# Rotary embedding: float32 transfers on the SyncE hardware queue, with ScalarE doing the casts

## The chip, the cores and the metric

The kernel runs on one core of a Trainium2 chip. The metric is the device time of one execution in microseconds (us). A profile's span is about 1.8 us shorter than the time of the same execution (317.2 us against 319.0 us for the kernel before), because the time also holds what lies outside the first and last recorded instruction.

## The reference

`x` has shape (8, 2048, 16, 64), in float32. The two halves of its last dimension are rotated by angles that depend on the sequence position alone:

```python
x1, x2 = x[..., :32], x[..., 32:]
out1 = x1 * cos - x2 * sin          # cos, sin: (2048, 32), broadcast over batch and heads
out2 = x1 * sin + x2 * cos
return np.concatenate([out1, out2], axis=-1).astype(np.float32)
```

The kernel must read 67.1 MB and write 67.1 MB of float32. There is very little arithmetic per byte, so the transfers will matter most.

## The kernel before

One tile holds a batch: 128 partitions x 16 positions x 16 heads x 64 values, in float16. GpSimd issues every transfer on its software queue, and the transfer itself casts between float32 in HBM and float16 in SBUF. VectorE works in place in float16. There are five such tiles.

```python
def load(b):
    xt = io_pool.tile([P, J, H, D], f16)                    # io_pool: bufs=5, J = 16
    nc.gpsimd.dma_start(out=xt, in_=x[b].rearrange("(p j) h d -> p (j h d)", j=J))
    return xt

def rotate(xt):
    for j0 in range(0, J, JC):                              # JC = 8
        # ... views x1, x2, sin_b, cos_b, xw; temporaries v1, v2
        nc.vector.tensor_mul(out=v1, in0=x2, in1=sin_b)
        nc.vector.tensor_mul(out=v2, in0=x1, in1=sin_b)
        nc.vector.tensor_mul(out=xw, in0=xw, in1=cos_b)     # both halves at once
        nc.vector.tensor_sub(out=x1, in0=x1, in1=v1)
        nc.vector.tensor_add(out=x2, in0=x2, in1=v2)

for b in range(B):
    tiles[b] = load(b)
    # ... the tables with b == 0
    if b >= 4:
        nc.gpsimd.dma_start(out=out[b - 4].rearrange(...), in_=tiles[b - 4])
    rotate(tiles[b])
# ... the last four stores
```

The build reorders what an engine has to do: it is not bound to the order of the program where no data depends on it.

## Time and profile before

| | before |
|---|---|
| time, median of 6 runs | 319.06 us (318.79 to 319.14) |
| span of the profiled run | 317.2 us |
| VectorE (DVE) busy | 210.7 us, 66% |
| transfers, share of 16 engines' span | 99.6% |
| HBM bytes over the span | 425 GB/s |

From the page of the kernel before: the span, the busy time of each engine with its share of the span and its number of instructions, the busy tenths of the transfers in 40 slices, then the queues with packets, MB and share of 16 engines.

```profile
span 317.2 us, 164 instructions
DVE 210.7 (66%) x80; POOL 9.9 (3%) x22
DMA  7979999999999999999999999999999999999996
q0 software_dynamic: 2592, 100.93, 99.6%
q14 instruction: 1, 0.01, 0.0%
HBM read 67.63 MB, written 67.11 MB: 425 GB/s over the span
```

The queue is full from end to end. Mind the MB column: a packet is counted by one side only, so a casting load counts its float16 bytes (33.5 MB) and a casting store its float32 bytes (67.1 MB). The HBM line counts float32 both ways.

The windows view of the same kernel, first and last stretch (window, length, busy time of VectorE and GpSimd with the number of instructions, clock, share of the transfers, GB/s):

```profile
0.00:20.00 20.00, 0.00 (x0) 4.05 (x11) 1.00 0.89 184
280.00:317.00 37.00, 0.00 (x0) 0.00 (x0) 1.00 0.93 397
```

Only about 2 us at the start (11% of 20) and 2.6 us at the end (7% of 37) are not streaming. Two waits (engine, line, what it waited for: us, times, longest) tell the rest:

```profile
POOL xt L37 <- DMA out_dram<-xt: 118.1, 3, 56.4
DVE v L55 <- DMA xt<-in_x_dram: 29.9, 2, 20.2
```

GpSimd stands in three waits for a store to land before it may load into that tile again, and VectorE waits for loads. Neither costs anything as long as the queue has work.

### The profile page before, as it was taken

The numbers are of one execution on the slowest core, as the hardware profiler recorded it, in microseconds if no ns is written. First come the engines' busy times: TensorE is split into PE (matmuls) and PEld (weight loads), VectorE is DVE, ScalarE is ACT, GpSimd is POOL, SyncE is SP. The second block draws the span as 40 slices with busy tenths as digits, with TensorE's granted clock in tenths as the row PEclk, the third lists the DMA queues.
The fourth block names the chain that finished last, engine by engine and source line by source line (L and its number), as shares of the span: only waits on it lengthen the run. The fifth ranks groups of instructions, "written<-read, shape, count | busy, mean of one in ns | idle before, by whom it ended". The sixth has DMA issues, their size and how long they took to land.

```text
span 317.2 us, 164 instructions
## 1 busy us (share of the span) xinstructions
DVE 210.7 (66%) x80; POOL 9.9 (3%) x22
## 2 busy tenths in 40 slices
DVE  0009999999999999999069999995009994000000
POOL 5000000000000000001000000100000000000000
DMA  7979999999999999999999999999999999999996
GB/s 132 256 163 266 207 198 202 260 198 198 198 264 264 397 397 529 397 331 231 231 198 199 380 413 397 454 471 264 198 314 413 397 446 479 397 397 512 413 397 264
DMA packets 2593, 100.93 MB, mean 318 GB/s; under 512 B 288, under 2 KB 544, under 8 KB 544
## 3 DMA queue, kind: packets, MB, share of 16 engines
q0 software_dynamic: 2592, 100.93, 99.6%
q14 instruction: 1, 0.01, 0.0%
HBM read 67.63 MB, written 67.11 MB: 425 GB/s over the span
## 4 chain that ended last, share of the span: by engine, by line
issue 34%; DMA 19%; DVE 16%; another core or an unknown queue 13%; POOL 1%; POOLq 0%; DVEq 0%; PEldq 0%
DMA xt<-in_x_dram 12%; DMA sin_sb<-in_sin_dram 7%; DVE xt L58 5%; DVE v L55 3%; DVE xt L60 3%; DVE v L56 3%; DVE xt L59 2%; POOL xt L37 1%; POOL out_dram L68 1%; POOLq L101 0%; POOLq L37 0%; POOLq L73 0%; DVEq L55 0%; PEldq L101 0%
## 5 line engine op out<-in xcount | busy, mean ns | idle before, releaser
L55 DVE TENSOR_TENSOR v<-xt,sin_sb 128x4096 f16<-128x4096 f16 x16 | 36.5, 2284 | 54.2 <-DMA xt<-in_x_dram 29.9
L58 DVE TENSOR_TENSOR xt<-xt,cos_sb 128x8192 f16<-128x8192 f16 x16 | 70.7, 4416 | 0.0
L59 DVE TENSOR_TENSOR xt<-xt,v 128x4096 f16<-128x4096 f16 x16 | 36.5, 2283 | 0.1
L60 DVE TENSOR_TENSOR xt<-xt,v 128x4096 f16<-128x4096 f16 x16 | 36.5, 2283 | 0.0
L56 DVE TENSOR_TENSOR v<-xt,sin_sb 128x4096 f16<-128x4096 f16 x16 | 36.5, 2283 | 0.0
L37 POOL DMA_DIRECT2D xt<-in_x_dram x8 | 4.4, 568 | 118.9 <-DMA out_dram<-xt 118.1
L68 POOL DMA_DIRECT2D out_dram<-xt x4 | 2.1, 539 | 73.8 <-DVE xt L60 73.8
L73 POOL DMA_DIRECT2D out_dram<-xt x4 | 2.1, 532 | 63.0 <-DVE xt L60 63.0
L44 POOL DMA_DIRECT2D cos_sb<-in_cos_dram x1 | 0.5, 548 | 0.0
L43 POOL DMA_DIRECT2D sin_sb<-in_sin_dram x1 | 0.5, 542 | 0.0
L90 POOL MEMSET const-float32-0.0<- 128x1 f32 x1 | 0.1, 100 | 0.2 <-issue 0.2
L90 POOL MEMSET const-bfloat16-1.0<- 128x1 bf16 x1 | 0.1, 103 | 0.0
L90 POOL MEMSET const-float32-1.0<- 128x1 f32 x1 | 0.1, 100 | 0.0
L90 POOL MEMSET const-uint8-127<- 128x1 uint8 x1 | 0.1, 100 | 0.0
## 6 DMA issues: line engine op xcount, KB each, us to landing
xt<-in_x_dram POOLq DMA_DIRECT2D x8, 4096.0 KB, 39.8
sin_sb<-in_sin_dram POOLq DMA_DIRECT2D x1, 128.0 KB, 22.2
cos_sb<-in_cos_dram POOLq DMA_DIRECT2D x1, 128.0 KB, 22.4
out_dram<-xt POOLq DMA_DIRECT2D x8, 65.9
```

The costliest lines, as they stand in the source:

```text
L37: nc.gpsimd.dma_start(out=xt, in_=x[b].rearrange("(p j) h d -> p (j h d)", j=J))
L43: nc.gpsimd.dma_start(out=sin_sb, in_=sin.rearrange("(p j) d -> p (j d)", j=J))
L44: nc.gpsimd.dma_start(out=cos_sb, in_=cos.rearrange("(p j) d -> p (j d)", j=J))
L55: nc.vector.tensor_mul(out=v1, in0=x2, in1=sin_b)
L56: nc.vector.tensor_mul(out=v2, in0=x1, in1=sin_b)
L58: nc.vector.tensor_mul(out=xw, in0=xw, in1=cos_b)
L59: nc.vector.tensor_sub(out=x1, in0=x1, in1=v1)
L60: nc.vector.tensor_add(out=x2, in0=x2, in1=v2)
L68: nc.gpsimd.dma_start(out=out[b - 4].rearrange("(p j) h d -> p (j h d)", j=J), in_=tiles[b - 4])
L73: nc.gpsimd.dma_start(out=out[b].rearrange("(p j) h d -> p (j h d)", j=J), in_=tiles[b])
L90: nc = _bacc.Bacc("TRN2", target_bir_lowering=False, num_devices=1)
```

## The change

The intent: the hardware queue in place of the software queue, plain float32 rows of 32 KB in place of casting rows of 64 KB, and the casts on ScalarE, which had nothing to do. Core of the diff:

```diff
-    JC = 8
+    JU = 8                                   # positions in a transfer: 32 KB rows, 4 MB tiles
+    JC = 4                                   # positions in a piece of compute
+    NBUF = 5
     def load(u):
-        xt = io_pool.tile([P, J, H, D], f16)
-        nc.gpsimd.dma_start(out=xt, in_=x[b].rearrange("(p j) h d -> p (j h d)", j=J))
+        xf = io_pool.tile([P, JU, H, D], f32)
+        nc.sync.dma_start(out=xf.rearrange("p j h d -> p (j h d)"), in_=rows(x, b, j0))
+    def narrow(c):                            # half_pool: bufs=3
+        xt = half_pool.tile([P, JC, H, D], f16)
+        nc.scalar.copy(out=xt.rearrange("p j h d -> p (j h d)"), in_=piece(c))
     # ... rotate: the same five VectorE operations, on half tiles of JC = 4
+    def widen(c):                             # back into the input tile
+        nc.scalar.copy(out=piece(c), in_=xt.rearrange("p j h d -> p (j h d)"))
+    # ... the first four loads and the tables, narrow(0)
+    for c in range(n * per):                  # n = 16 units, per = 2 pieces each
+        if c + 1 < n * per:
+            narrow(c + 1)
+        rotate(c)
+        widen(c)
+        if c % per == per - 1:
+            u = c // per
+            if u + NBUF - 1 < n:
+                tiles[u + NBUF - 1] = load(u + NBUF - 1)   # waits until store(u - 1) has landed
+            store(u, tiles[u])
```

More of the change, by code (lines that the diff above doesn't have):

```diff
@@ L20 @@
     f16 = mybir.dt.float16
+    f32 = mybir.dt.float32
     B, S, H, D = x.shape
@@ L25 @@
     J = S // P
-    JC = 8
+    JU = 8
+    JC = 4
+    NBUF = 5
     const_pool = ctx.enter_context(tc.tile_pool(name="rope_const", bufs=1))
-    io_pool = ctx.enter_context(tc.tile_pool(name="rope_io", bufs=5))
-    tmp_pool = ctx.enter_context(tc.tile_pool(name="rope_tmp", bufs=2))
+    io_pool = ctx.enter_context(tc.tile_pool(name="rope_io", bufs=NBUF))
+    half_pool = ctx.enter_context(tc.tile_pool(name="rope_half", bufs=3))
+    tmp_pool = ctx.enter_context(tc.tile_pool(name="rope_tmp", bufs=1))
@@ L32 @@
+    cos_f = const_pool.tile([P, J, Dh], f32)
+    sin_f = const_pool.tile([P, J, Dh], f32)
     cos_sb = const_pool.tile([P, J, Dh], f16)
     sin_sb = const_pool.tile([P, J, Dh], f16)
-    def load(b):
-        xt = io_pool.tile([P, J, H, D], f16)
-        nc.gpsimd.dma_start(
-            out=xt, in_=x[b].rearrange("(p j) h d -> p (j h d)", j=J)
-        )
-        return xt
-    def tables():
-        nc.gpsimd.dma_start(out=sin_sb, in_=sin.rearrange("(p j) d -> p (j d)", j=J))
-        nc.gpsimd.dma_start(out=cos_sb, in_=cos.rearrange("(p j) d -> p (j d)", j=J))
@@ L46, in rotate @@
-    def rotate(xt):
-        for j0 in range(0, J, JC):
-            js = slice(j0, j0 + JC)
-            v1 = tmp_pool.tile([P, JC, H, Dh], f16)
-            v2 = tmp_pool.tile([P, JC, H, Dh], f16)
-            x1 = xt[:, js, :, 0:Dh]
-            x2 = xt[:, js, :, Dh:D]
-            sin_b = sin_sb[:, js, :].unsqueeze(2).to_broadcast([P, JC, H, Dh])
-            cos_b = cos_sb[:, js, :].unsqueeze(2).to_broadcast([P, JC, 2 * H, Dh])
-            nc.vector.tensor_mul(out=v1, in0=x2, in1=sin_b)
-            nc.vector.tensor_mul(out=v2, in0=x1, in1=sin_b)
-            xw = xt[:, js, :, :].rearrange("p j h (e d) -> p j (h e) d", d=Dh)
-            nc.vector.tensor_mul(out=xw, in0=xw, in1=cos_b)
-            nc.vector.tensor_sub(out=x1, in0=x1, in1=v1)
-            nc.vector.tensor_add(out=x2, in0=x2, in1=v2)
@@ L62 @@
-    tiles = {}
-    for b in range(B):
-        tiles[b] = load(b)
-        if b == 0:
-            tables()
-        if b >= 4:
-            nc.gpsimd.dma_start(
-                out=out[b - 4].rearrange("(p j) h d -> p (j h d)", j=J), in_=tiles[b - 4]
-            )
-        rotate(tiles[b])
-    for b in range(B - 4, B):
-        nc.gpsimd.dma_start(
-            out=out[b].rearrange("(p j) h d -> p (j h d)", j=J), in_=tiles[b]
-        )
+    units = [(b, j0) for b in range(B) for j0 in range(0, J, JU)]
@@ new lines, in rows, with load, store @@
+    def rows(t, b, j0):
+        return t[b].rearrange("(p j) h d -> p j (h d)", j=J)[:, j0 : j0 + JU, :].rearrange(
+            "p j f -> p (j f)"
+        )
+    def load(u):
+        b, j0 = units[u]
+        xf = io_pool.tile([P, JU, H, D], f32)
+        nc.sync.dma_start(out=xf.rearrange("p j h d -> p (j h d)"), in_=rows(x, b, j0))
+        return xf
+    def store(u, xf):
+        b, j0 = units[u]
+        nc.sync.dma_start(out=rows(out, b, j0), in_=xf.rearrange("p j h d -> p (j h d)"))
@@ new lines, with piece, rotate @@
+    n = len(units)
+    per = JU // JC
+    tiles = {}
+    halves = {}
+    def piece(c):
+        u, k = divmod(c, per)
+        return tiles[u][:, k * JC : (k + 1) * JC, :, :].rearrange("p j h d -> p (j h d)")
+    def narrow(c):
+        xt = half_pool.tile([P, JC, H, D], f16)
+        nc.scalar.copy(out=xt.rearrange("p j h d -> p (j h d)"), in_=piece(c))
+        halves[c] = xt
+    def rotate(c):
+        u, k = divmod(c, per)
+        j0 = units[u][1] + k * JC
+        js = slice(j0, j0 + JC)
+        xt = halves[c]
+        v1 = tmp_pool.tile([P, JC, H, Dh], f16)
+        v2 = tmp_pool.tile([P, JC, H, Dh], f16)
+        x1 = xt[:, :, :, 0:Dh]
+        x2 = xt[:, :, :, Dh:D]
+        sin_b = sin_sb[:, js, :].unsqueeze(2).to_broadcast([P, JC, H, Dh])
+        cos_b = cos_sb[:, js, :].unsqueeze(2).to_broadcast([P, JC, 2 * H, Dh])
+        nc.vector.tensor_mul(out=v1, in0=x2, in1=sin_b)
+        nc.vector.tensor_mul(out=v2, in0=x1, in1=sin_b)
+        xw = xt.rearrange("p j h (e d) -> p j (h e) d", d=Dh)
+        nc.vector.tensor_mul(out=xw, in0=xw, in1=cos_b)
+        nc.vector.tensor_sub(out=x1, in0=x1, in1=v1)
+        nc.vector.tensor_add(out=x2, in0=x2, in1=v2)
@@ new lines, in widen @@
+    def widen(c):
+        xt = halves.pop(c)
+        nc.scalar.copy(out=piece(c), in_=xt.rearrange("p j h d -> p (j h d)"))
+    for u in range(NBUF - 1):
+        tiles[u] = load(u)
+        if u == 0:
+            nc.sync.dma_start(out=sin_f, in_=sin.rearrange("(p j) d -> p j d", j=J))
+            nc.sync.dma_start(out=cos_f, in_=cos.rearrange("(p j) d -> p j d", j=J))
+            nc.scalar.copy(out=sin_sb, in_=sin_f)
+            nc.scalar.copy(out=cos_sb, in_=cos_f)
+    narrow(0)
+    for c in range(n * per):
[8 more added lines that the diff above has]
+            store(u, tiles[u])
```

## The prediction

> **What bounds the kernel now.** The transfers. The page's queue section gives the one software queue 99.6% of 16 engines' span; VectorE is busy 210.7 of 317.2 us (66%). HBM reads and writes are 67.63 + 67.11 MB, 425 GB/s over the span. About 2 us at the start (window 0 to 20 us: DMA share 0.89) and 2.6 us at the end (280 to 317: 0.93) are not streaming, so while streaming it moves about 134.7 MB in 313 us = 430 GB/s. The Trainium skill, "DMA: Bandwidth & Descriptors", section "Where 436 GB/s comes from", puts the ceiling of the 16 ports at 435 GB/s. The trace agrees: the kernel sits 1% below it. VectorE's waits (54 us) are off the critical path.
>
> **What the change removes.** The cast in the transfer and GpSimd's work, but no HBM byte: x and out were float32 in HBM before. On the SBUF side the bytes double, but the float32 side already set the pace (loads and stores both run near 430 GB/s counted in float32: 240 to 280 us shows 436 GB/s, mostly stores). So the gain is at most that 1%, plus about 1 us of start.
>
> **What it adds.** ScalarE: 32 narrowings and 32 widenings of 128x4096. No trace has one; the Trainium skill, "ScalarE: Activation LUTs", section "What ACT_TABLE_LOAD costs", gives 186 ns + 0.833 ns per element, an estimate of 3.6 us each, 230 us in all. VectorE keeps 211 us: per 4 MB unit 13.2 us on VectorE, 14.4 us on ScalarE, against 2 x 4.19 MB / 430 GB/s = 19.5 us of transfer. Compute stays hidden.
>
> **What it moves: the risk.** Half as much is in flight: five tiles of 4 MB, not 8. Load u+5 must wait until store u has landed, on the same in-order SyncE queue as the stores. If the build puts load u+5 ahead of store u+1, as the program has it, then SyncE stands in that wait while store u+1 is ready, and the queue runs empty at each of 11 loads. Each costs landing + issue + first byte, by the start and end losses above about 2.3 us: 25 us, 340 us in all. If the order is store u+1 first (before's trace shows such a reordering: stores 0 and 1 both were issued before load 5), a store covers each wait and nothing is lost: 315 to 318 us. I give both about half, with mixtures between them.
>
> Start: first 4 MB land at 12 us, tables follow, first store at about 35 us while five loads stream until about 52 us; no hole. End: behind the last load about four stores (39 us) cover the last unit's 20 us of compute; no hole.
>
> **Prediction:** 320 us, range 312 to 343; faster by over 2% 0.09, within 2% 0.54, slower by over 2% 0.37.
>
> **What would show each step.** DMA queue: one hardware queue with 134 MB at 96 to 100% of the span if right. ScalarE busy near 230 us, a narrowing 3.6 us; VectorE unchanged at 211 us. Issues: the order of loads and stores on SyncE, and in the waits how long SyncE stands for stores; DMA share near 0.98 or near 0.9 (holes).
>
> **What would make it wrong.** The hardware queue with float32 on both sides streams clearly slower or faster than 430 GB/s; table transfers in tiny pieces (several us at the start); ScalarE, in order, stands at a narrowing whose load hasn't landed while a widening is ready, so that stores come late; copies above 4.8 us, when ScalarE would set the pace.

## More of the kernel before

The trace has a record for each row that a DMA engine moves. The records do not name the engine: a row is joined to the one whose end meets its start, and the spacing is the mean over rows that nothing delays (how the delayed ones are left out moves it by about half a nanosecond). A row of 64 KB (float32 side) starts 2412.8 ns after the one before it on its engine. Sixteen engines at that pace move 16 x 65,536 B / 2412.8 ns = 435 GB/s. The Trainium skill, "DMA: Bandwidth & Descriptors", section "Where 436 GB/s comes from", gives 435 GB/s as the ceiling of the 16 ports; the trace agrees.

## The result, and the profile after

| | before | after |
|---|---|---|
| time, median of 6 runs | 319.06 us | 321.52 us (320.18 to 321.71) |
| ratio, 95% interval | | 1.0067 (1.0047 to 1.0086) |

A ratio is the mean time of one kernel's fast runs over the mean of the other's in the same rounds, so it is not quite the ratio of the medians. The change makes the kernel slower by a small amount that is clear of noise. The runs of after fall in two groups, 320.2 to 320.4 us (two) and 321.5 to 321.7 us (four). The trace kept is one of the first group (span 318.6 us).

The page of the kernel after, the lines that answer to those above:

```profile
span 318.6 us, 387 instructions
DVE 223.2 (70%) x160; ACT 229.3 (72%) x67; POOL 0.2 (0%) x4
DMA  8999999999999999999999999999999999999994
q1 hardware_dynamic: 4896, 134.74, 98.7%
q14 instruction: 3, 0.02, 0.0%
HBM read 67.63 MB, written 67.11 MB: 423 GB/s over the span
```

The queue is still full, now with plain float32 bytes. The costliest groups of after (busy us, mean ns of one, then idle before them and what ended it):

```profile
L92 ACT CAST xf<-xt 128x4096 f32<-128x4096 f16 x32 | 115.3, 3604 | 51.0 <-DVE xt L88 28.0
L69 ACT CAST xt<-xf 128x4096 f16<-128x4096 f32 x32 | 114.5, 3600 | 18.7 <-DMA xf<-in_x_dram 18.7
```

A cast takes 3.60 us. The Trainium skill, "ScalarE: Activation LUTs", section "What ACT_TABLE_LOAD costs", gives 186 ns + 0.833 ns per element for an ACTIVATE with immediate scale and bias, which is 3598 ns for 4096; the trace, which calls the operation CAST, agrees. ScalarE's 229 us and VectorE's 223 us both stay under the transfers.

The order of issue was the disputed step. Timeline of SyncE in after (start, length of the group from its first to its last issue, line, what, how many):

```profile
2.11 2.01 SPq L51 DMA_DIRECT2D xf<-in_x_dram  x4
34.91 18.17 SPq L56 DMA_DIRECT2D out_dram<-xf  x2
63.52 10.26 SPq L51 DMA_DIRECT2D xf<-in_x_dram  x2
73.87 4.33 SPq L56 DMA_DIRECT2D out_dram<-xf  x2
102.56 10.13 SPq L51 DMA_DIRECT2D xf<-in_x_dram  x2
112.74 1.09 SPq L56 DMA_DIRECT2D out_dram<-xf  x2
```

The build issues in pairs: stores 0 and 1, then loads 5 and 6, and so on. Load 5 waits for store 0, but store 1 is then already in the queue, and load 6 waits for store 1 while load 5 is under way. So SyncE's waits are long, but the queue holds work throughout. The windows view of after, in columns as above with ScalarE added, shows no hole between the ends:

```profile
160.00:210.00 50.00, 34.53 (x25) 38.87 (x11) 0.00 (x0) 1.00 1.00 431
210.00:260.00 50.00, 38.38 (x29) 38.80 (x11) 0.00 (x0) 1.00 1.00 434
310.00:318.00 8.00, 0.00 (x0) 0.00 (x0) 0.00 (x0) 1.00 0.58 250
```

The last window, with 0.58 of 16 engines busy, does not set after apart: before has 0.50 in the same window.

**Where the time came from.** The ends of single engines show it. A transfer ends with 16 marks in the trace, one from each DMA engine. The last transfer of before has its first and last mark 0.62 us apart; the last of after has them 2.65 us apart. At the end of after, 15 engines have ended their last row by 315.60 us and one ends its last row at 317.35 us, a row and a half later. I call such an engine a straggler. The kernel ends with its slowest engine. Worked out from the two profiled runs (span 317.2 and 318.6 us):

| term | before | after | difference |
|---|---|---|---|
| first row starts, us from the span's start | 2.61 | 1.74 | -0.9 |
| 128 x 64 KB: row spacing 2412.8 ns, or 2 x 1209.7 ns | 308.8 | 309.7 | +0.9 |
| first to last mark of the last transfer | 0.62 | 2.65 | +2.0 |
| last mark to end of span | 1.5 | 0.9 | -0.6 |
| sum of these | | | +1.4 |

The spans differ by 1.4 us. These terms are not the whole span: they leave 3.7 us over in each kernel, which hold the tables (about 1.3 us) and what all engines lose at their first rows and at the first stores. So the question for the experiments is what makes the straggler.

### The profile page after: what moved, and what is told of

Read it like the earlier page. It is cut to its first block, busy times and chain, and to the rows that moved or that the text cites. A ratio compares the mean times of both kernels' runs of the same rounds, so it can differ in the third digit from the quotient of the medians.

```text
span 318.6 us, 387 instructions
## 1 busy us (share of the span) xinstructions
DVE 223.2 (70%) x160; ACT 229.3 (72%) x67; POOL 0.2 (0%) x4
## 4 chain that ended last, share of the span: by engine, by line
DMA 51%; ACT 7%; DVE 4%; issue 2%; SPq 1%; DVEq 0%; ACTq 0%
DMA out_dram<-xf 45%; DMA xf<-in_x_dram 6%; ACT xf L92 3%; ACT xt L69 3%; DVE xt L86 1%; DVE xt L87 1%; DVE v L83 1%; DVE v L84 1%; DVEq L138 0%; SPq L51 0%; SPq L56 0%; DVE xt L88 0%; ACTq L92 0%
## 5 line engine op out<-in xcount | busy, mean ns | idle before, releaser
L92 ACT CAST xf<-xt 128x4096 f32<-128x4096 f16 x32 | 115.3, 3604 | 51.0 <-DVE xt L88 28.0
L69 ACT CAST xt<-xf 128x4096 f16<-128x4096 f32 x32 | 114.5, 3600 | 18.7 <-DMA xf<-in_x_dram 18.7
L83 DVE TENSOR_TENSOR v<-xt,sin_sb 128x2048 f16<-128x2048 f16 x32 | 39.1, 1223 | 70.6 <-ACT xt L69 53.6
L86 DVE TENSOR_TENSOR xt<-xt,cos_sb 128x4096 f16<-128x4096 f16 x32 | 73.3, 2292 | 1.2
L87 DVE TENSOR_TENSOR xt<-xt,v 128x2048 f16<-128x2048 f16 x32 | 39.2, 1225 | 1.1
L84 DVE TENSOR_TENSOR v<-xt,sin_sb 128x2048 f16<-128x2048 f16 x32 | 39.0, 1218 | 0.0
L88 DVE TENSOR_TENSOR xt<-xt,v 128x2048 f16<-128x2048 f16 x32 | 39.0, 1218 | 0.0
```

Of the source, the lines that this page charges most:

```text
L69: nc.scalar.copy(out=xt.rearrange("p j h d -> p (j h d)"), in_=piece(c))
L92: nc.scalar.copy(out=piece(c), in_=xt.rearrange("p j h d -> p (j h d)"))
```

## The experiments

In what follows, marks that are "x us apart" are the first and last mark of the last transfer. First theory A: the transfers bind; the loss is the smaller rows and a straggler that the longer program's instruction fetches make (the transfers of 8 KB on the queue that the page calls instruction, q14 above: three in after, one in before). Rival B: compute is late and leaves holes. Each timed run has a 95% interval of at most 0.25% to either side, against the kernel before of the same rounds.

### e1: less compute

```diff
-        nc.vector.tensor_mul(out=v1, in0=x2, in1=sin_b)
-        nc.vector.tensor_mul(out=v2, in0=x1, in1=sin_b)
         nc.vector.tensor_mul(out=xw, in0=xw, in1=cos_b)
-        nc.vector.tensor_sub(out=x1, in0=x1, in1=v1)
-        nc.vector.tensor_add(out=x2, in0=x2, in1=v2)
```

> The changed kernel with one of VectorE's five operations (the cosine product), so a wrong result on purpose; VectorE's busy time falls from 223 to about 75 us and its program from 162 to about 34 instructions. Theory A (the transfers bind; the loss is made of row pieces of 32 KB, about 1 us, and of one DMA engine of the 16 that ends 1.8 us behind the others, late because the instruction fetches of a longer program fall on it): transfers as before, 128 x 2.42 us per engine; fewer fetches than the 3 of the changed kernel, last engine under 1 us behind, 318 to 321 us. Theory B (stores come late, because they wait for rotate and widen, and leave holes): the holes go, 314 to 316 us.

Measured: 320.79 us (319.08 to 321.49), ratio 1.0047. VectorE fell from 223 to 73 us and the time by less than 1 us. Rival B is out: taking away two thirds of VectorE's work returns next to nothing. From its page:

```profile
span 317.5 us, 238 instructions
DVE 73.3 (23%) x32; ACT 227.3 (72%) x67; POOL 0.2 (0%) x4
q1 hardware_dynamic: 4896, 134.74, 99.1%
```

There were two fetches, and the last transfer's marks lay 1.44 us apart in place of 2.65; theory A had expected less than 1.

### e2: pieces of half the size

```diff
-    JC = 4
+    JC = 2
```

> Pieces of half the size (JC 2): the same bytes and transfers, twice the compute instructions (320 on VectorE, 128 on ScalarE). Theory A: ScalarE 242 us, VectorE 245 us, both under the 315 us of transfers, so no loss from them; about twice the 3 instruction fetches, so the last engine ends 1 to 2 us further behind: 321.5 to 324 us. If the fetches have nothing to do with the straggler: 320.2 to 321.7 us, as the changed kernel.

Measured: 322.31 us, ratio 1.0105; VectorE 239 us, ScalarE 242 us, four fetches; marks 4.90 us apart. In the range of theory A. But one fetch more moved the marks by 2.25 us, which is much for a record of 0.3 us. The marks of each transfer in turn show part of it: they widen by 0.7 us across the fetch at 57.1 us and by 1.0 us across the one at 238.1 us. e6 puts a price on a fetch.

### e3: rows of 16 KB

```diff
-    JU = 8
-    NBUF = 5
+    JU = 4
+    NBUF = 10
```

> Rows of 16 KB, ten tiles of 2 MB in place of five of 4 MB. Theory A: a row costs a fixed part; before moved 64 KB in 2411 ns start to start and the changed kernel two rows of 32 KB in 2419 ns, so four rows of 16 KB should take 2435 ns, 128 times that is 2 us more: 322.5 to 324 us. If 32 KB rows cost nothing by themselves: 320 to 322 us.

Measured: 330.47 us, ratio 1.0362: a miss. The row's fixed cost is only part of it: rows start 607 ns apart, so 64 KB take 2428 ns against 2419 ns, and 128 times 9 ns is 1.2 us. But the change did more than I meant. The windows view of e3 near its end:

```profile
300.00:312.00 12.00, 8.29 (x7) 8.32 (x4) 0.00 (x0) 1.00 1.01 431
312.00:318.00 6.00, 5.65 (x4) 2.61 (x2) 0.00 (x0) 1.00 0.70 296
318.00:324.00 6.00, 0.00 (x0) 3.40 (x1) 0.00 (x0) 1.00 0.62 262
```

With the queue nearly empty, the last two stores come late behind their widenings (ScalarE starts its last two at 310.80 and 317.80 us), and all engines have two holes of about 2.1 us. Rows also took longer in many places than their usual 611 ns (mean 627 ns, which is 8 us over the 512 rows of an engine). The marks show where. Averaged over the 16 engines, the transfer that ends a pair of loads, just before stores follow, lands 0.2 to 1.4 us late at each of eleven places about 20 us apart, 6.6 us in all; in after the same sum over six places is about 0.6 us. So the two holes (4.1 us) and these losses are the larger part of e3's 9 us over after, and the size of the row is the smaller. Why halving the transfers made all engines lose there is not shown.

### e4: the order that the prediction feared

```diff
+        with tc.issue_after(issued[-1].ins):       # each store behind the load before it
             nc.sync.dma_start(out=rows(out, b, j0), in_=xf.rearrange(...))
```

> Forces the issue order that the prediction feared: each store behind the load that the program has ahead of it, so SyncE stands in the wait of load u+5 while store u+1 is ready. Both theories: 11 holes. By the prediction's estimate of 2.3 us each 25 us more, 345 us, DMA busy near 91% of the span. If the queue isn't drained (stores late anyway), under 330 us.

Measured: 362.07 us, ratio 1.1347. The waits of SyncE and the queue in e4:

```profile
SPq L53 <- DMA out_dram<-xf: 253.0, 11, 28.4
```

```profile
q1 hardware_dynamic: 4896, 134.74, 93.0%
```

All 11 holes are there, at (362.07 - 321.52) / 11 = 3.7 us each. The row records of a typical one: the last row of a store ends at 86.54 us, the store's last mark is at 86.88, SyncE issues at 86.89, the next rows start at 87.85 and the first takes about 1.9 us instead of 1.2. The mean start of a row is late by 1.9 us at the first row and by 0.6 at the second, 2.5 us together: close to the 2.3 us that I took from the ends of before. Another 1.3 us come where the short queue goes from that load to its store (0.5 and 0.8 us on the mean engine); this cycle is 3.8 us longer than one without a hole. So the mechanism was right, and its price was too low by this second part.

### e5: the software queue put back

```diff
-        nc.sync.dma_start(...)        # x, out, cos, sin
+        nc.gpsimd.dma_start(...)
```

> The changed kernel with every transfer issued by GpSimd (software queue), still float32 and 32 KB rows: the queue alone is put back. If the loss of the changed kernel is its hardware queue: back to 318.5 to 319.5 us, last engine under 0.7 us behind, as before. If it is the rows of 32 KB and the instruction fetches: not faster than the changed kernel, and the start 0.9 us later: 321 to 323 us.

Measured: 324.93 us, ratio 1.0185; marks 4.30 us apart. The hardware queue is not what costs time: without it the kernel is slower still, by more than I expected. The two profiled spans differ by 4.1 us: the first row starts 0.9 us later, the marks lie 1.7 us further apart, and from the last mark to the end of the span it takes 2.1 us in place of 0.9.

### e6: more instruction fetches, and nothing else

```diff
         rotate(c)
+        for _ in range(20):
+            nc.gpsimd.memset(scratch, 0.0)       # one column that nobody reads
         widen(c)
```

> The changed kernel plus 640 memsets of one column on GpSimd, which nothing waits for: transfers, ScalarE's and VectorE's programs unchanged; about 5 instruction fetches of 8 KB more than the 3 of the changed kernel, in the first 65 us. If a fetch costs the DMA engine that serves it about 1 us and that engine is the last: last engine 5 to 9 us behind, 324 to 328 us. If e2's loss came from its smaller pieces, or a fetch costs only the 0.3 us of its record: 320.2 to 322 us.

Measured: 322.99 us, ratio 1.0125, under the range: a half miss. There were eight fetches:

```profile
q14 instruction: 8, 0.07, 0.1%
```

The marks of the transfers widen right where the fetches are: from 0.94 to 1.57 us across the one at 31.3 us (after has 0.48 us there), from 1.55 to 2.73 us across the one at 51.3 us, whose record is the longest with 0.94 us (after goes from 0.48 to 0.54 us there), and from 3.25 to 3.91 us across two at 91.4 and 92.0 us. At the end they are 4.74 us apart, 2.1 us more than in after for five additional fetches. So a fetch can put an engine back by 0.3 to 1.1 us. It shows in the marks only where it meets an engine that is among the last: those of e6 at 179.0 and 294.7 us widen the marks by less than 0.1 us.

The same reading of after and e1, which issue in the same order: the marks of e1 go from 0.42 to 1.44 us, and its two fetches (204.7 and 286.2 us) widen them by no more than 0.05 us. So about 1.0 us of spread comes without fetches. Those of after go from 0.49 to 2.65 us. Its fetch at 292.5 us takes them from 1.89 to 2.68; the one at 91.7 us falls in a stretch where they widen by 0.5 us, against 0.2 us in e1; the one at 179.0 us does nothing. Of the 2.2 us by which the marks of after widen, an estimate from these numbers gives about half to fetches and half to something else. The next runs show what that is.

### c32 and c64: the copy alone, rows of 32 and 64 KB

Both only copy x to out through float32 tiles on the hardware queue: no tables, no compute, a wrong result. In all the copies each issue is pinned behind the one before it (`tc.issue_after`), so the order is that of the program.

```diff
+    # c32: JU = 8, NBUF = 5 (4 MB tiles)        c64: JU = 16, NBUF = 3 (8 MB tiles)
+    tiles = {u: load(u) for u in range(NBUF)}
+    store(0)
+    for u in range(1, n):
+        store(u)
+        if u - 1 + NBUF < n:
+            tiles[u - 1 + NBUF] = load(u - 1 + NBUF)
```

> Copy of x to out through SBUF alone (wrong result on purpose): float32, hardware queue, rows of 32 KB, five tiles of 4 MB, no tables (1.3 us of transfer less), next to no compute program, so 0 or 1 instruction fetches. Theory A: rows start to start 1209.5 ns, last engine under 0.7 us behind, 316 to 318 us. If the hardware queue makes a straggler by itself: still 1.5 us or more behind, 319 us or more.

> The same copy with rows of 64 KB and three tiles of 8 MB. Theory A (a row has a fixed cost of about 8 ns): 2411 to 2413 ns start to start instead of 2 x 1209.5, 1 us less than the 32 KB copy: 315 to 317 us. If the row size costs nothing: same as the 32 KB copy within 0.3 us.

Measured: c32 320.32 us (marks 3.91 us apart), c64 318.70 us (marks 3.07). Neither has a single instruction fetch, and both have stragglers. Theory A falls as the whole cause: there is another source. The row records say where. In c64 the rows of some engines are late by 0.2 to 0.8 us at 120, 159, 198, 238 and 277 us, every 39 us. These are the places where the queue goes from a load to a store (the marks of load 3 end at 120.7 us, those of load 4 at 159.6 us). Where it goes from a store to a load, half way between, little is lost (at most 0.44 us, on one engine at 181 us). In after such losses come near 92, 131, 170 and 209 us, every 39 us, at the end of each pair of loads. Row size by itself: 2 x 1209.5 = 2419.0 against 2414.2 ns, so 0.6 us over 128.

Theory C: at a turn from load to store some engines lose a few tenths of a microsecond, and never catch up. With the cast the SBUF side moves half the bytes, and this hides the turn. That the cast hides it is tested next; that the halved bytes are the reason is not.

### c64g, and the cast with five and with three tiles

```diff
-        nc.sync.dma_start(...)                     # c64
+        nc.gpsimd.dma_start(...)                   # c64g: the same copy on the software queue
-        xf = io_pool.tile([P, JU, H, D], f32)      # c64g
+        xf = io_pool.tile([P, JU, H, D], f16)      # casting copies, NBUF = 5 and NBUF = 3
```

> The 64 KB copy (float32, three tiles of 8 MB) issued by GpSimd in place of SyncE. Theory C (new, after the copies on the hardware queue showed stragglers of 3 to 4 us without any instruction fetch: where the queue turns between loads and stores, float32 on both sides makes some engines lose 0.2 to 0.5 us each time; with the cast the SBUF side moves half the bytes and hides it): as on the hardware queue, stalls every 39 us, last landing 2 to 4 us behind the first, 319 to 322 us with a start 0.9 us later. If the stalls belong to the hardware queue: under 0.7 us behind, 318 us or less.

> The same copy with float16 tiles, so the transfers cast as those of the kernel before, five tiles. Theory C: no stalls at the turns, last landing under 0.7 us behind the first, 315.5 to 317.5 us, 2 us or more under the float32 copy on the same queue. If the cast has nothing to do with it: within 0.5 us of the float32 copy on this queue.

Measured: float32 320.53 us (marks 3.22 us apart), casting with five tiles 317.49 us (marks 0.69). But five tiles also allow fewer turns (4 from load to store in place of 6) and a deeper queue than three. The control with three tiles has the same transfers in the same order as c64g; only the tile's type differs.

> The casting copy with three tiles instead of five, so that its 16 transfers stand in the same order, with the same number of turns and the same depth of queue, as those of the float32 copy on GpSimd (320.53 us); the tile type is the only difference. Theory C (float32 on both sides makes the stalls at the turns): no stalls behind the first one, last landing under 0.8 us behind the first, 317.3 to 318.0 us. Rival D (fewer turns or a deeper queue were what helped the five-tile copy, not the cast): last landing 2 to 3.5 us behind the first, 319.5 us or more.

Measured: 317.65 us, ratio to before 0.9961 (0.9947 to 0.9974); marks 0.73 us apart. Rival D falls. The windows of the float32 copy on GpSimd (window, length, GpSimd, clock, share of the transfers, GB/s):

```profile
308.00:312.00 4.00, 0.00 (x0) 1.00 1.02 442
312.00:316.00 4.00, 0.00 (x0) 1.00 0.23 98
```

and of the casting copy with the same order:

```profile
308.00:312.00 4.00, 0.00 (x0) 1.00 1.22 524
312.00:316.00 4.00, 0.00 (x0) 1.00 0.01 0
```

In the float32 copy a few engines still run when most have ended; the casting copy stops at once. In the row records of c64g one engine is late by 0.6 us at 199, 1.0 us at 239 and 0.9 us at 279 us. In the casting copy no engine is late by as much as 0.2 us after the first turn at 62 us, where all 16 lose about 1.1 us with the cast and 1.3 us without, on average. The row spacing differs by only 1.4 ns (2414.2 and 2412.8), 0.2 us in all.

### c32g3: the same copy, turning less often

```diff
-    store(0)
-    for u in range(1, n):
-        store(u)
-        if u - 1 + NBUF < n:
-            tiles[u - 1 + NBUF] = load(u - 1 + NBUF)
+    for g in range(0, n, 3):
+        for u in range(g, min(g + 3, n)):
+            store(u)
+        for u in range(g + NBUF, min(g + NBUF + 3, n)):
+            tiles[u] = load(u)
```

> The 32 KB copy on the hardware queue with stores and loads in threes rather than one by one: a third of the turns. Theory C: last landing 1 to 2 us behind the first instead of 3.9, 318 to 319.3 us against 320.3. If the turns have no part: 320 to 320.6 us.

Measured: 317.23 us against 320.32 us for c32; marks 0.91 us apart in place of 3.91. The queues of c32 and of c32g3, same bytes and packets:

```profile
q1 hardware_dynamic: 4608, 134.22, 98.4%
```

```profile
q1 hardware_dynamic: 4608, 134.22, 99.2%
```

With 5 turns from load to store in place of 12 the straggler goes, and with it 3.1 us, somewhat more than I expected. The range said a third; it is 5 of 12. The grouping also puts more transfers in the queue ahead of each turn, so the number of turns and the depth of the queue are not told apart here.

### The copies side by side

| kernel | queue | in SBUF | row | turns, load to store | fetches | marks of the last transfer apart | median |
|---|---|---|---|---|---|---|---|
| cast, 3 tiles | GpSimd | float16 | 64 KB | 6 | 0 | 0.73 us | 317.65 us |
| c64g | GpSimd | float32 | 64 KB | 6 | 0 | 3.22 us | 320.53 us |
| c64 | SyncE | float32 | 64 KB | 6 | 0 | 3.07 us | 318.70 us |
| c32 | SyncE | float32 | 32 KB | 12 | 0 | 3.91 us | 320.32 us |
| c32g3 | SyncE | float32 | 32 KB | 5 | 0 | 0.91 us | 317.23 us |
| before | GpSimd | float16 | 64 KB | 3 | 1 | 0.62 us | 319.06 us |
| after | SyncE | float32 | 32 KB | 7 | 3 | 2.65 us | 321.52 us |

Read from the top, each step is one part of the change: float32 in SBUF +2.9 us, the hardware queue -1.8 us, rows of 32 KB with more turns +1.6 us. A grouped order gives 3.1 us back. Some of these runs were made in different rounds and on different chips; by their ratios to the kernel before of the same rounds (318.8 to 319.0 us) the steps are +2.6, -1.6, +1.5 and -2.8 us. What the hardware queue gains lies mostly at the ends: in c64 the first row starts 0.9 us earlier than in c64g, and the span ends 0.6 us sooner after the last mark. The kernels at the bottom also load the tables (0.5 MB, about 1.3 us at this rate) and have a program to fetch. No version that computes the result and beats before was found. A grouped order in the kernel itself was not run, because even a copy that computes nothing is at most 0.6% faster than before. So that grouping would help the computing kernel is not shown.

## Why the prediction was right or wrong

- **"What bounds the kernel now: the transfers."** Right. In e1 VectorE lost two thirds of its work and the time moved by less than 1 us.
- **"So the gain is at most that 1%."** Right, and nothing of it came. The start was 0.9 us earlier as foreseen, but a row pair of 32 KB costs 2419.4 ns in place of 2412.8 (+0.9 us).
- **"ScalarE: an estimate of 3.6 us each, 230 us in all."** Right: 3.60 us and 229.3 us. VectorE has 223 us, not 211: an operation on half the elements took 1.22 us, more than half of 2.28 us.
- **"Compute stays hidden."** Right (e1).
- **The order of issue.** I gave each order about half. The build chose neither of the two as I drew them, but pairs, which belong to the good branch: a transfer covers each wait.
- **"Nothing is lost: 315 to 318 us."** This is the term that was mis-sized. That order gave 320.2 to 321.7 us. The sum treated 16 engines as one queue with one rate. The rate between the ends was right (431 to 434 GB/s), but the kernel ends with its slowest engine, and with float32 on both sides single engines fall behind at turns from load to store (c64g against the casting copy, +2.9 us) and at instruction fetches (0.3 to 1.1 us each where they meet a late engine, e6). In the trace of after, where the marks end 2.65 us apart, the two share about equally by the estimate above (e6).
- **"Each costs about 2.3 us: 340 us in all."** The mechanism was right, the size was not: 3.7 us each and 362 us (e4). The hole itself took 2.5 us; the turn from load to store in a short queue, which I had not counted, took 1.3 us.
- **The middle and the range.** 320 us with "within 2%" as the likeliest held, but partly by luck: 320 us was the middle of two branches, 315 to 318 and 340 us, and each of them was too low.

Open: why a turn from load to store costs an engine time when both sides carry float32, and why few engines and not all; why one fetch costs the last engine a microsecond (e2 at 238.1 us) and another nothing; which engines they are (the records do not name them); whether fewer turns or a deeper queue made c32g3 fast, and whether a grouped order would help the kernel that computes; and what the four slower runs of after have more (1.2 us), since the trace kept is of the faster group.

## What to carry to other kernels

Moving the cast from the transfer to an idle engine did not speed up a kernel that already moved its HBM bytes at 425 GB/s; the cast was free there, and it even hid the turns from loads to stores. When a queue is full at 98 to 99%, look at how far apart the 16 engines end the last transfer, because the kernel ends with the slowest one. In a copy, loads and stores in groups kept them together (0.91 against 3.91 us); in the kernel, five fetches more drove them apart (4.74 against 2.65 us). Before fearing or dismissing a reordering of waits on an in-order queue, read the built order: here it decided between 322 and 362 us.

## What the Trainium skill lacked or had wrong

- "DMA: Bandwidth & Descriptors", section "Latency and other measured facts": it reports that engines 7 and 15 are usually slower and calls that specific to the software queue. Here the float32 copy has late engines on the hardware queue too (marks 3.07 us apart, c64), and the casting copy on the software queue has none (0.73 us). Which engines are late the records do not name, so this does not test the page's statement about those two.
- The same page, section "SWDGE vs HWDGE vs iDMA", on the cast: it says that a cast needs the software queue, but not what it costs in rate. Here it costs nothing: 64 KB of float32 in 2412.8 ns on an engine, 435 GB/s over 16, against 2414.2 ns without the cast.
- The same page, section "Issuing engine by pattern", calls the hardware queue generally faster. On the same float32 copy it was, by 1.8 us of 320 (c64 against c64g); that did not make the kernel with it faster than the casting kernel.
- No page that I read has the cost of turning between loads and stores (0.2 to 1.0 us on single engines from load to store, float32 on both sides), or what an instruction fetch costs the transfers beside it (8 KB, a record of mostly 0.31 us, up to 1.1 us of delay on an engine, e6).
- "DMA: Bandwidth & Descriptors", section "Anatomy of one DMA — SWDGE (gpsimd) path", gives about 2 us for the fixed part of a transfer on the software queue. On the hardware queue, one that ran dry cost 2.5 us in e4, and 1.3 us more at the turn that followed.
